# A hand-ordered attention schedule: weighing behind the copies, another order of products, a buffer for compressed-value weights

## The chip, the cores and the metric

The kernel runs on one core of a Trainium2 chip. Its time is the device time of one execution in microseconds (us); with one core there is nothing to take a maximum over. PE is TensorE, DVE is VectorE, ACT is ScalarE, POOL is GpSimd; SP issues the large loads.

## The reference, cut to what matters

256 tokens of width 1024, all in float32. First two layers of feed-forward, a mixer of two kinds of attention, feed-forward; then two layers of a hybrid attention and a feed-forward:

```python
def hybrid_mixer(h, w_in, ...):                 # "mixer"
    proj = h @ w_in                             # q, six key/value parts, gates, moba q k v
    kc = gelu(blocks(k_cmp) @ w_ck1) @ w_ck2    # compressed keys, values alike with w_cv1, w_cv2
    o_nsa  = g0 * attn(q, kc, vc) + g1 * attn(q_rot, k_slc, v_slc) + g2 * attn(q_rot, k_win, v_win)
    o_moba = attn(rope(q_m), rope(k_m), v_m)
    return concatenate([o_nsa, o_moba]) @ w_out

def hybrid_layer(x, ...):                       # "hybrid"
    aq, ak, av, iq, ik, iw, bq, bk, bv, gates = split_cols(rms_norm(x) @ w_in)
    ya = sparse_attention(rope(norm(aq)), rope(norm(ak)), av, top-k of an index score)
    yb = differential attention: (p0 - lam * p1) @ bv, then a norm
    x = x + (sigmoid(g_a) * (ya @ w_up_a) + sigmoid(g_b) * (yb @ w_up_b)) @ w_out
    return x + (silu(gate) * up) @ w_ffn_out
```

## The kernel before, in words

The activations stay on the chip, 314 MB of weights stream through it once. A weight chunk of 1 MB (512 input rows by 512 columns) is loaded by SP into one of three `raw` buffers; ACT rounds each half into `hi` and DVE forms `lo` as raw less hi (four buffers each); a product is then three matmuls, hi by the activation's high part, lo by high, hi by low (L210 to L212 in the mixers, L252 to L257 towards the residual, L312 and L316 in the feed-forward). A `raw` buffer is free for the next load once DVE has made the second `lo` of it. SP works its queue in order, so a load that waits for a buffer holds back all behind it.

In the feed-forward parts a scheduler orders the instructions. In the mixers (about 211 to 405 and 778 to 972 us of the trace) and the hybrids (1157 to 1395 and 1585 to 1825 us) the order on PE, ACT, DVE and POOL is that of the program's text (`manual_schedule`). There a list of products, `Fill` (L1580), is handed out between the steps of the attention: `fill.us(t)` issues products worth t us, by a planner's own figures; `fill.until(name)` issues them until the named product is done; `fill.later(t, f)` issues f when t us of the plan have gone by. `Fill.split` issues the roundings and the loads of the chunks ahead.

A mixer begins with `cmp_blocks` (L747), which copies compressed keys and values into `kd`, turns them on PE and adds positions into `fl`; `compress` (L781) multiplies `fl` by two loaded halves of w_ck1 and of w_cv1, in `raw` buffers, without rounding (L807). `keys` turns the selected and the window keys (`kt`), `heads_T` (L405) turns heads four at a time, `cmp_probs` (L865) makes the compressed attention's weights. Then `pipeline` (L500) walks over slots, 12 in a mixer and 8 in a hybrid (4 of differential attention, 4 of sparse). A slot has four steps:

- scores (`scores_exp`, L415): PE makes two score tiles and adds a mask; four times DVE takes a row maximum (`nm`, L436) and ACT the exponential (`P`, L439).
- weigh: DVE makes the factor `c` and scales `P` (L478, L479; in the differential slots L1271, L1272).
- turn (`p_T`, L443): PE transposes `P`, six times in a mixer slot; ACT copies two thirds to `PT` (L453), DVE one third (L458).
- values: PE multiplies `PT` by the values (L493, L495; in the differential slots from L1283).

The scores run two slots ahead of the values; `post` names further work behind a slot's values. In a round the old `pipeline` issues turn(n), products f1, values(n), post, scores(n+2), products f2, weigh(n+2), products f3.

## Time and profile before

| | |
|---|---|
| median of 3 runs | 2021.23 us (2019.96 to 2023.68) |
| the profiled execution's own time | 2026.66 us |
| its span | 2025.0 us |
| mean granted clock of PE | 0.960 |
| busy: PE, DVE, ACT, POOL | 1863.4, 1318.4, 1003.2, 577.3 us |
| loaded | 314 MB, 155 GB/s over the span |

The span is what the trace shows; the time also holds what lies around it (1.7 us here). PE is busy for 92% of the span, so 8% of it is what its waits can give, and the granted clock says how fast it was while busy: 1.00 is 2.4 GHz, 0.50 is 1.2 GHz. The rows that the prediction uses are quoted in a section of their own below.

### The profile page before, as it was taken

Reading aid. Unit: us, or ns where it says so; the run is one execution under the profiler, and the core shown is the slowest. Engines: PE = TensorE matmul, PEld = TensorE weight load, DVE = VectorE, ACT = ScalarE, POOL = GpSimd, SP = SyncE. Lnnn points to the kernel's source line nnn. Section 1 sums busy time; section 2 is a strip of 40 time slices with the busy share of each in tenths; the row PEclk is TensorE's granted clock in tenths of the full one; section 3 lists DMA queues with packets and bytes.
Section 4 is the critical chain, followed back from the end, with each engine's and each line's share of the span. In section 5 each row is a group of like instructions: output and inputs, shape, how many; then the busy total and the mean of one; then the engine's idle time right before and its main releaser. Section 6 shows DMA issues by size and latency. Waiting matters only on the chain.

```text
span 2025.0 us, 27057 instructions
## 1 busy us (share of the span) xinstructions
PE 1863.4 (92%) x10136; PEld 1547.9 (76%) x10136; DVE 1318.4 (65%) x2202; ACT 1003.2 (50%) x1948; POOL 577.3 (29%) x628
## 2 busy tenths in 40 slices
PE   8899788899999998878999998799999997899999
PEld 7788665688888887656888876687887776788887
DVE  7765445687667665346776588556866696567763
ACT  6554424555555554235655444445555444546552
POOL 5450110044315421100454144001542252013540
PEclk9899899999999999889999999899999998999999
DMA  7546432355655464412555544236546443245543
GB/s 247 184 146 210 153 120 63 105 187 157 228 177 175 159 229 148 147 42 83 189 178 182 184 137 145 84 105 208 167 145 229 152 146 104 84 162 193 169 164 125
DMA packets 149075, 314.40 MB, mean 155 GB/s; under 512 B 5588, under 2 KB 30320, under 8 KB 148944
## 3 DMA queue, kind: packets, MB, share of 16 engines
q1 hardware_dynamic: 148016, 311.15, 46.7%
q0 software_dynamic: 896, 1.52, 0.4%
q8 instruction: 79, 1.29, 0.3%
q14 instruction: 52, 0.43, 0.1%
q10 hardware_dynamic: 32, 0.01, 0.0%
HBM read 311.61 MB, written 1.05 MB: 154 GB/s over the span
## 4 chain that ended last, share of the span: by engine, by line
PE 65%; DVE 15%; ACT 9%; POOL 5%; issue 5%; DMA 2%; ACTq 0%; POOLq 0%; DVEq 0%
PE acc L312 10%; PE acc L253 7%; PE acc L257 7%; PE acc L252 7%; PE acc L316 5%; PE psS L312 5%; DVE lo L1578 4%; ACT P L439 3%; PE acc L210 3%; PE psT L312 2%; PE acc L212 2%; DVE lo L190 2%; PE acc L211 2%; PE psS L316 2%; PE psO L312 2%
## 5 line engine op out<-in xcount | busy, mean ns | idle before, releaser
L190 DVE TENSOR_TENSOR lo<-raw,hi 128x1024 fp32r<-128x1024 f32 (+2 forms) x436 | 535.3, 1254 | 158.6 <-ACT hi L189 153.7
L189 ACT ACTIVATE hi<-raw 128x1024 fp32r<-128x1024 f32 (+2 forms) x436 | 423.4, 999 | 150.0 <-PE acc L257 107.5
L312 PE MATMUL acc<-xx,hi 128*128 128x512 f32 x1056 | 376.8, 401 | 9.8 <-DVE gcol L139 7.4
L316 PE MATMUL acc<-xx,lo 128*128 128x256 f32 x1056 | 294.3, 281 | 0.0
L312 PEld LDWEIGHTS acc<-xx,hi 128*128 128x128 f32 x1056 | 199.6, 190 | 58.5 <-DVE gcol L139 7.7
L1578 DVE TENSOR_TENSOR lo<-raw,hi 128x1024 fp32r<-128x1024 f32 (+1 forms) x168 | 204.3, 1229 | 47.4 <-ACT hi L1577 47.2
L253 PE MATMUL acc<-lo,gh 128*128 128x512 f32 x528 | 209.7, 397 | 1.5 <-DVE lo L190 1.5
L252 PE MATMUL acc<-hi,gh 128*128 128x512 f32 x528 | 209.1, 396 | 0.0
L316 PEld LDWEIGHTS acc<-xx,lo 128*128 128x128 f32 x1056 | 200.6, 190 | 1.2
L312 PE MATMUL psS<-xx,hi 128*128 128x512 f32 x528 | 192.6, 398 | 2.2 <-ACT hi L189 2.2
L341 POOL TENSOR_TENSOR g<-g,rbc 128x256 f32<-128x256 f32 x132 | 136.0, 1044 | 181.8 <-DVE g L326 123.9
L353 POOL TENSOR_TENSOR hh<-g,u 128x256 f32<-128x256 f32 x132 | 138.0, 1053 | 162.1 <-DVE u L326 161.4
L257 PE MATMUL acc<-hi,gl 128*128 128x512 f32 x528 | 173.6, 395 | 0.0
L210 PE MATMUL acc<-hi,xx 128*128 128x512 f32 (+2 forms) x416 | 170.6, 411 | 1.6 <-ACT xx L1514 1.6
L1577 ACT ACTIVATE hi<-raw 128x1024 fp32r<-128x1024 f32 (+1 forms) x168 | 167.4, 1035 | 4.4 <-PE acc L212 4.2
L212 PE MATMUL acc<-hi,xx 128*128 128x512 f32 (+2 forms) x416 | 161.6, 388 | 0.8 <-DVE xx L1515 0.8
L211 PE MATMUL acc<-lo,xx 128*128 128x512 f32 (+2 forms) x416 | 161.3, 388 | 0.0
L351 POOL TENSOR_TENSOR g<-g,rbc 128x256 f32<-128x256 f32 x132 | 134.5, 1024 | 66.8 <-DVE g L344 66.8
L316 PE MATMUL psS<-xx,lo 128*128 128x256 f32 x528 | 149.2, 282 | 1.9 <-DVE lo L190 1.9
L223 ACT ACTIVATE gh<-hh 128x256 fp32r<-128x256 f32 x132 | 55.1, 418 | 172.4 <-POOL hh L353 172.1
L344 DVE SCALAR_TENSOR_TENSOR g<-th,g 128x256 f32<-128x256 f32 x132 | 82.4, 628 | 74.9 <-ACT th L343 74.9
L343 ACT ACTIVATE th<-g 128x256 f32<-128x256 f32 x132 | 54.8, 417 | 152.7 <-POOL g L341 152.4
(431 smaller groups left out, 3672.9 us busy)
## 6 DMA issues: line engine op xcount, KB each, us to landing
raw<-in_w_in_dram SPq DMA_DIRECT2D x60, 1024.0 KB, 5.1
raw<-in_w_ffn_down_dram SPq DMA_DIRECT2D x44, 1024.0 KB, 4.9
raw<-in_w_ffn_up_dram SPq DMA_DIRECT2D x40, 1024.0 KB, 5.1
raw<-in_w_ffn_in_dram SPq DMA_DIRECT2D x40, 1024.0 KB, 5.3
raw<-in_w_ffn_gate_dram SPq DMA_DIRECT2D x39, 1024.0 KB, 5.2
raw<-in_w_ffn_out_dram SPq DMA_DIRECT2D x22, 1024.0 KB, 5.1
raw<-in_w_out_dram SPq DMA_DIRECT2D x12, 1024.0 KB, 4.9
raw<-in_w_ffn_gate_dram SPq DMA_DIRECT2D x10, 512.0 KB, 3.8
```

Of the source, the lines that this page charges most:

```text
L189: nc.scalar.activation(hi[:, hs], raw[:, hs], AF.Copy),
L190: nc.vector.tensor_tensor(lo[:, hs], raw[:, hs], hi[:, hs].bitcast(F32), op=ALU.subtract),
L210: mm(out, ah, bh, start=start, stop=False)
L211: mm(out, ah, bl, start=False, stop=False)
L212: self.last = mm(out, al, bh, start=False, stop=stop)
L252: mm(accs[t, n], ah, hi[:, j, cs], start=k == 0, stop=False)
L253: mm(accs[t, n], ah, lo[:, j, cs], start=False, stop=False)
L257: mm(accs[t, n], al, hi[:, j, cs], start=False, stop=k == nk - 1)
L312: nc.tensor.matmul(banks[j], hi[:, k, fs], xk.rearrange("p u s -> p (u s)"), start=h == 0 and k == 0, stop=False,)
L316: self.last = nc.tensor.matmul(banks[j][:, 0:S], lo[:, k, fs], xk[:, 0, :], start=False, stop=h == 1 and k == 3,)
L1577: nc.scalar.activation(self.hi[:, hs], self.raw[:, hs], AF.Copy)
L1578: nc.vector.tensor_tensor(self.lo[:, hs], self.raw[:, hs], self.hi[:, hs].bitcast(F32), op=ALU.subtract)
```

## The change

`pipeline` now issues scores(n+1), products, then turn(n), weigh(n+1), products f1, values(n), post, scores(n+2), products f2: the weighing of the next slot stands behind this slot's copies of `PT` on DVE, where before the weighing of the slot after next stood ahead of the next slot's copies. The mixer projects `q` first and `kw` second (before: `kw`, `q`); the second key transpose and the second step of the compressed probabilities are done behind the first slot's scores (`pre`); the turns of `mq` and `mk` stand one slot later. w_cv1 gets a buffer of its own, `cv1`, one for both layers, and its first half is asked for before the hand-ordered part begins. In the hybrid `broadcast` is issued 8 us of the plan later, the index transposes 1 us later and with 3.2 us of products behind them instead of 2.0, the turns of `xa` 5 us later, those of `xk` behind the values of slots 0 and 1. Products whose inputs are not there yet are held back by a `ready` test instead of by their place. `Fill` looks 3 halves ahead at first and then 5 (before: 6). `kd`, `zr` and `pc` share one buffer instead of two, `u` shares that of `hs`, `e`. All instructions are the same in number on PE, DVE, ACT and POOL.

```diff
@@ -278,9 +278,10 @@
-        if fill:
+        if ready:
             return [
-                (None, [Chunk(self, rows(c), [2, D])], 16, lambda hl, c=c: run(c, hl[0]), None) for c in range(nch)
+                (None, [Chunk(self, rows(c), [2, D])], 16, lambda hl, c=c: run(c, hl[0]), None, lambda c=c: ready(c))
+                for c in range(nch)
             ], end
@@ -497,24 +498,31 @@
-    def pipeline(self, fill, slots, post, f1, f2, f3):
-        for n in range(2):
-            slots[n][0]()
-            fill.tick(0.85)
-            fill.us(2.2)
-            slots[n][1]()
-        fill.us(0.6)
+    def pipeline(self, fill, slots, post, f1, f2, pre=None):
+        slots[0][0]()
+        fill.tick(0.85)
+        fill.us(2.8)
+        if pre is not None:
+            pre()
+            fill.tick(0.2)
+            fill.us(0.7)
+        slots[0][1]()
+        slots[1][0]()
+        fill.tick(0.85)
+        fill.us(1.6)
         for n, (_, _, turn, values) in enumerate(slots):
...
             fill.tick(0.45 if rest else 0.65)
-            fill.us(f1)
             if rest:
+                fill.us(1.4)
                 rest()
                 fill.tick(0.2)
-                fill.us(0.9)
+            if n + 1 < len(slots):
+                slots[n + 1][1]()
+            fill.us(1.0 if rest else f1)
             values()
@@ -524,9 +532,6 @@
             fill.us(f2 - 0.4 if rest else f2)
-            if n + 2 < len(slots):
-                slots[n + 2][1]()
-            fill.us(f3 - 0.5 if rest else f3)
@@ -652,6 +657,7 @@
+                        tok["n"] = r + 1
@@ -660,13 +666,16 @@
+                def end(o):
+                    self.split(oh[:, 4 + k, :], ol[:, 4 + k, :], o[:, 0:256])
+                    tok["n"] = 5 + k
...
-                    self.caus, plain, self.psO,
-                    lambda o: self.split(oh[:, 4 + k, :], ol[:, 4 + k, :], o[:, 0:256]),
+                    self.caus, plain, self.psO, end,
@@ -682,64 +691,62 @@
             out, out_end = self.to_residual(
-                lambda k: oh[:, k, :], lambda k: ol[:, k, :], out_rows, KT, 1.0, after, held=1, fill=True
+                lambda k: oh[:, k, :], lambda k: ol[:, k, :], out_rows, KT, 1.0, after, held=1,
+                ready=lambda c: tok.get("n", 0) >= 2 * c + 2 or c == 3,
             )
             fill = Fill([
+                self.proj_item("q", w_in, 0, 512, pr, queries),
                 self.proj_item("kw", w_in, 1024, 280, pr, windows),
-                self.proj_item("q", w_in, 0, 512, pr, queries),
                 self.proj_item("mq", w_in, 1304, 512, pr, moba_in("mq", True)),
                 self.proj_item("mk", w_in, 1816, 512, pr, moba_in("mk", True)),
...
             fill.prime()
+            next(comp)
             es.enter_context(tc.manual_schedule(engines=MANUAL))
             rope2(kv[:, :, 256:384])
...
             fill.us(2.5)
             next(blocks)
-            fill.until("kw")
+            fill.us(1.6)
             next(blocks, None)
-            next(comp)
-            fill.us(4.5)
+            fill.us(3.6)
             next(comp)
             fill.until("q")
...
             fill.us(0.7)
             next(kt_)
-            fill.us(0.7)
-            next(kt_)
             qT, qrT, mq, mk = (mp.tile([128, 4, S], F32, tag="T4", name=n, bufs=4) for n in ("qT", "qrT", "mqT", "mkT"))
-            fill.us(0.7)
+            fill.us(1.1)
             q = tok["q"]
             self.heads_T(qT, q, 0, self.psT, 0.125)
...
             q4 = q.rearrange("p t (h d) -> p t h d", h=8)
             self.rope_part(mp, q4, q4, 8)
-            fill.us(1.0)
+            fill.us(2.0)
             next(comp)
             next(comp)
             fill.us(1.2)
             next(comp)
-            fill.us(2.6)
+            fill.us(1.8)
+            fill.until("kw")
             next(comp, None)
             self.heads_T(qrT, q, 0, self.psT, 0.125)
             self.heads_T(qrT, q, 1, self.psO, 0.125)
-            fill.us(1.0)
             probs = self.cmp_probs(mp, cp, qT, kcb, gt, tok)
-            next(probs)
-            fill.us(1.2)
+            fill.us(0.7)
             next(probs)
...
             post = {
                 0: lambda: next(probs, None),
-                2: lambda: self.heads_T(mq, tok["mq"], 0, self.psT, 0.125),
-                3: lambda: self.heads_T(mq, tok["mq"], 1, self.psT, 0.125),
-                4: lambda: self.heads_T(mk, tok["mk"], 0, self.psT),
-                5: lambda: self.heads_T(mk, tok["mk"], 1, self.psT),
+                3: lambda: self.heads_T(mq, tok["mq"], 0, self.psT, 0.125),
+                4: lambda: self.heads_T(mq, tok["mq"], 1, self.psT, 0.125),
+                5: lambda: self.heads_T(mk, tok["mk"], 0, self.psT),
+                6: lambda: self.heads_T(mk, tok["mk"], 1, self.psT),
             }
-            self.pipeline(fill, slots, post, 1.3, 1.1, 0.8)
+            self.pipeline(fill, slots, post, 1.8, 1.4, lambda: (next(probs), next(kt_)))
             fill.all()
             es.close()
@@ -747,17 +754,14 @@
-        kds = []
...
-            kd = mp.tile([128, 2, 2, 2, 64], F32, tag="c2", name="kd", bufs=2)
+            kd = mp.tile([128, 2, 2, 2, 64], F32, tag="c2", name="kd")
...
-            kds.append(kd)
-        for i, kd in enumerate(kds):
@@ -791,10 +795,10 @@
         def fetch(h):
-            return [
-                self.wraw(a[n][l][h * 1024 : (h + 1) * 1024, :].rearrange("(j p) f -> p j f", p=128), [8, 256])
-                for n in ("w_ck1", "w_cv1")
-            ]
+            src = [a[n][l][h * 1024 : (h + 1) * 1024, :].rearrange("(j p) f -> p j f", p=128) for n in ("w_ck1", "w_cv1")]
+            w = mp.tile([128, 8, 256], F32, name="cv1", bufs=1)
+            nc.sync.dma_start(w, src[1])
+            return [self.wraw(src[0], [8, 256]), w]
@@ -823,7 +827,7 @@
-        u = mp.tile([128, 128], F32, name="u")
+        u = mp.tile([128, 256], F32, tag="hs", name="u")[:, 0:128]
@@ -843,7 +847,7 @@
-        zr = mp.tile([128, 2, 2, 2, 32], F32, tag="c2", name="zr", bufs=2)
+        zr = mp.tile([128, 2, 2, 2, 32], F32, tag="c2", name="zr")
@@ -892,7 +896,7 @@
-        pc = cp.tile([128, 2, 8, 32], F32, tag="c2", name="pc", bufs=2)
+        pc = cp.tile([128, 2, 8, 32], F32, tag="c2", name="pc")
@@ -1078,7 +1082,6 @@
             ix = evac(ps, 324, "ix")
-            pr.broadcast()
             ikd = mp.tile([128, 2, 2, 64], F32, name="ikd")
@@ -1343,11 +1346,11 @@
                 fs = slice(f % 4, f % 4 + 2)
-                self.split(mh[f // 4][:, fs, :], ml[f // 4][:, fs, :], m)
+                fill.later(2.0, lambda: self.split(mh[f // 4][:, fs, :], ml[f // 4][:, fs, :], m))
...
                 lambda k: mh[k // 4][:, k % 4, :], lambda k: ml[k // 4][:, k % 4, :], a["w_out_2"][l], KT,
-                0.5, after, held=1, fill=True,
+                0.5, after, held=1, ready=lambda c: True,
             )
@@ -1361,21 +1364,23 @@
                 gate(1, 1, lambda: gate_b(1)),
-                up(ub, 0, lambda: tok["ybh"], lambda: tok["ybl"], up_b),
-                up(ub, 1, lambda: tok["ybh"], lambda: tok["ybl"], up_b),
-                up(ua, 0, lambda: yah, lambda: yal, up_a),
-                up(ua, 1, lambda: yah, lambda: yal, up_a),
+                up(ub, 0, lambda: tok["ybh"], lambda: tok["ybl"], up_b, lambda: "y" in tok),
+                up(ub, 1, lambda: tok["ybh"], lambda: tok["ybl"], up_b, lambda: "y" in tok),
+                up(ua, 0, lambda: yah, lambda: yal, up_a, lambda: "ya" in tok),
+                up(ua, 1, lambda: yah, lambda: yal, up_a, lambda: "ya" in tok),
             ] + out)
...
             es.enter_context(tc.manual_schedule(engines=MANUAL))
+            fill.later(8.0, pr.broadcast)
             fill.later(2.5, lambda: index_rope(0))
...
             fill.until("xb")
+            fill.us(1.0)
             index_T()
             fill.tick(0.65)
-            fill.us(2.0)
+            fill.us(3.2)
             for _ in index_scores():
@@ -1389,20 +1394,24 @@
             fill.until("xk")
-            fill.us(1.0)
+            fill.us(6.0)
             self.heads_T(aqT, tok["xa"], 0, self.psT, 0.125)
...
             fill.until("bv")
-            fill.us(0.5)
-            self.heads_T(akT, tok["xk"], 0, self.psT)
-            self.heads_T(akT, tok["xk"], 1, self.psO)
             slots = [diff(h) for h in range(4)] + [sparse(k) for k in range(4)]
-            self.pipeline(fill, slots, {3: norm_y}, 1.3, 1.3, 1.3)
+            post = {
+                0: lambda: self.heads_T(akT, tok["xk"], 0, self.psT),
+                1: lambda: self.heads_T(akT, tok["xk"], 1, self.psT),
+                3: norm_y,
+            }
+            self.pipeline(fill, slots, post, 1.8, 1.8)
             fill.us(2.0)
...
                 fill.tick(0.45)
-                fill.us(1.2)
+                if t == 0:
+                    fill.us(1.2)
+            tok["y"] = tok["ya"] = True
             fill.all()
@@ -1589,12 +1598,12 @@
             self.upto.append(self.upto[-1] + 2 * len(it[1]))
-        self.pos, self.now, self.debt = 0, 0.0, 0.0
+        self.pos, self.ahead, self.now, self.debt = 0, 3, 0.0, 0.0
         self.i, self.gen, self.n, self.past, self.tasks = 0, None, 0, set(), []
...
         while self.pos < min(upto, len(self.halves)):
-            for c, _ in self.halves[self.pos : self.pos + 6]:
+            for c, _ in self.halves[self.pos : self.pos + self.ahead]:
                 c.ask()
@@ -1602,6 +1611,7 @@
         self.split(self.upto[1])
+        self.ahead = 5
@@ -1640,17 +1652,20 @@
         self.debt += t
-        while self.debt > 0 and self.step():
-            pass
+        while self.debt > 0:
+            if not self.step():
+                self.tick(self.debt)
+                self.debt = 0.0
...
         while name not in self.past:
-            self.step()
+            assert self.step()
         self.debt = 0.0
...
             pass
+        assert self.i == len(self.items)
         self.tick(1e9)
```

On SP, in the mixer of layer 0 (`raw` from in_w_in is a chunk of the projections, 280 columns for `kw`, from in_w_ck and in_w_cv a half of a compression weight). Before:

```order
L175 DMA raw<-in_w_in_dram 128x4x280 x2
L175 DMA raw<-in_w_in_dram 128x4x512 x5
L175 DMA raw<-in_w_ck_dram 128x8x256
L175 DMA raw<-in_w_cv_dram 128x8x256
L175 DMA raw<-in_w_ck_dram 128x8x256
L175 DMA raw<-in_w_cv_dram 128x8x256
L175 DMA raw<-in_w_in_dram 128x4x512 x3
```

and now:

```order
L175 DMA raw<-in_w_in_dram 128x4x512 x4
L175 DMA raw<-in_w_in_dram 128x4x280
L175 DMA raw<-in_w_ck_dram 128x8x256
L175 DMA raw<-in_w_in_dram 128x4x280
L175 DMA raw<-in_w_in_dram 128x4x512 x2
L800 DMA cv_2233<-in_w_cv_dram 128x8x256
L175 DMA raw<-in_w_ck_dram 128x8x256
L175 DMA raw<-in_w_in_dram 128x4x512 x4
```

The first half of w_ck1 moved ahead of the second chunk of `kw` and of both chunks of `mq`; the second halves (L800 and the row behind it) now stand behind the two chunks of `mq`. The first half of w_cv1 is gone from here: it is SP's seventh load at the start of the program, between two loads of the first feed-forward; that of layer 1 stands among the loads of w_out of layer 0.

On DVE, in slots of the mixer of layer 0 in which moba heads are turned (`nm` belongs to scores, `c` and `P` to weigh, `PT` to turn, `lo` to the next product's chunk, `ol` to the slot's result). Before:

```order
L458 COPY PT<-psO 128x2x128
L1578 TENSOR_TENSOR lo<-raw,hi 128x1024
L224 TENSOR_TENSOR ol<-psO,oh 128x256
L436 TENSOR_REDUCE nm<-psS 128x1 x4
L635 TENSOR_SCALAR c<-sm 128x4
L636 RECIPROCAL c<-c 128x4
L478 TENSOR_SCALAR P<-P,c 128x256 x2
L479 TENSOR_TENSOR P<-P,c 128x2x128
L458 COPY PT<-psO 128x2x128
```

and now:

```order
L459 COPY PT<-psO 128x2x128
L640 TENSOR_SCALAR c<-sm 128x4
L641 RECIPROCAL c<-c 128x4
L479 TENSOR_SCALAR P<-P,c 128x256 x2
L480 TENSOR_TENSOR P<-P,c 128x2x128
L224 TENSOR_TENSOR ol<-psO,oh 128x256
L437 TENSOR_REDUCE nm<-psS 128x1 x4
L1587 TENSOR_TENSOR lo<-raw,hi 128x1024
L459 COPY PT<-psO 128x2x128
```

Between the maxima `nm` and the next copy `PT` stood the four rows of the weighing; now one rounding, `lo`, stands there, and the weighing behind the copy.

On PE, in the hybrid of layer 0, the turns of `xk` and the scores behind them (L428 and L430 before, L429 and L431 now). Before:

```order
L212 MATMUL acc<-hi,xx 128x512
L410 MATMUL psT<-ident,xk 128x128 x4
L410 MATMUL psO<-ident,xk 128x128 x4
L428 MATMUL psS<-bkT,bqT 128x256 x2
L430 MATMUL psS<-bkT,bqT 128x128 x2
```

and now:

```order
L1286 MATMUL psO<-tok,PT 128x128
L1287 MATMUL psO<-tok,PT 128x128
L1288 MATMUL psO<-tok,PT 128x128
L411 MATMUL psT<-ident,xk 128x128 x4
L429 MATMUL psS<-bkT,bqT 128x256 x2
L431 MATMUL psS<-bkT,bqT 128x128 x2
```

The turns stood ahead of the first slot; each of the two now follows the values of a slot.

## Rows read from the trace of the kernel before

**Rows 1.** The page's first part: busy time, share of the span, instructions of each engine.

```profile
PE 1863.4 (92%) x10136; PEld 1547.9 (76%) x10136; DVE 1318.4 (65%) x2202; ACT 1003.2 (50%) x1948; POOL 577.3 (29%) x628
```

**Rows 2.** Four stretches: us, busy PE PEld DVE ACT POOL, PE clock, DMA share, GB/s.

```profile
239.20:252.90 13.70, 6.21 (x36) 3.10 (x37) 1.10 (x1) 0.00 (x0) 0.00 (x0) 0.50 0.53 164
283.00:400.00 117.00, 92.79 (x503) 66.69 (x503) 65.59 (x163) 54.00 (x145) 4.89 (x8) 0.91 0.25 77
1239.30:1246.20 6.90, 5.41 (x15) 4.49 (x16) 6.53 (x12) 2.88 (x5) 4.21 (x6) 0.51 0.48 158
1261.00:1330.00 69.00, 52.94 (x349) 45.48 (x348) 39.18 (x100) 32.80 (x101) 1.85 (x2) 0.88 0.21 69
```

**Rows 3.** What PE waited for, 211 to 405 us: us, times, longest.

```profile
PE psO L493 <- DVE PT L458: 16.1, 6, 4.9
PE psS L807 <- DMA raw<-in_w_ck_dram: 9.2, 1, 9.2
PE psS L807 <- DMA raw<-in_w_cv_dram: 2.9, 1, 2.9
```

**Rows 4.** The same, 778 to 972 us.

```profile
PE psS L807 <- DMA raw<-in_w_ck_dram: 9.1, 1, 9.1
```

**Rows 5.** The same, 1150 to 1395 us.

```profile
PE psO L1283 <- DVE PT L458: 10.6, 4, 4.7
PE psO L493 <- DVE PT L458: 5.1, 3, 2.6
PE psS L1130 <- ACT iT L1114: 2.6, 1, 2.6
PE psO L410 <- DVE xa L1005: 2.2, 1, 2.2
PE psO L410 <- DVE xk L1005: 2.2, 1, 2.2
PE psT L410 <- DVE xa L1005: 1.6, 1, 1.6
```

**Rows 6.** Timeline of DVE in one mixer slot: start, us, line, operation, [idle before].

```profile
332.65 0.29 DVE L436 TENSOR_REDUCE nm<-psS 128x1 f32<-128x128 f32 x1 [0.65 <-ACT P L439]
334.41 1.23 DVE L1578 TENSOR_TENSOR lo<-raw,hi 128x1024 fp32r<-128x1024 f32 x1 [1.47 <-ACT hi L1577]
335.55 0.16 DVE L635 TENSOR_SCALAR c<-sm 128x4 f32<-128x4 f32 x1
337.02 0.42 DVE L458 COPY PT<-psO 128x256 f32<-128x256 f32 x1
```

**Rows 7.** Timeline of ACT in the same slot.

```profile
333.33 1.04 ACT L1577 ACTIVATE hi<-raw 128x1024 fp32r<-128x1024 f32 x1
334.28 0.57 ACT L453 COPY PT<-psT 128x512 f32<-128x512 f32 x1
```

**Rows 8.** Timeline of PE, products at either clock.

```profile
1245.51 0.63 PE L210 MATMUL acc<-hi,xx 128*128 128x512 f32 x1
1245.94 0.50 PE L211 MATMUL acc<-lo,xx 128*128 128x512 f32 x1
1246.51 0.40 PE L210 MATMUL acc<-hi,xx 128*128 128x512 f32 x1
1246.75 0.40 PE L211 MATMUL acc<-lo,xx 128*128 128x512 f32 x1
```

**Rows 9.** Timeline of SP's queue, layer 0 mixer.

```profile
238.06 0.37 SPq L175 DMA_DIRECT2D raw<-in_w_ck_dram  x1
240.33 0.37 SPq L175 DMA_DIRECT2D raw<-in_w_cv_dram  x1
```

**Rows 10.** DMA issues, 190 to 280 us: xcount, KB each, median us to landing.

```profile
raw<-in_w_in_dram SPq DMA_DIRECT2D x8, 1024.0 KB, 5.2
```

**Rows 11.** DMA from 0 to 34 us: rate in 40 equal slices, and one group of issues.

```profile
GB/s 0 0 194 274 296 357 371 376 293 256 374 400 388 367 386 386 392 225 207 267 217 142 164 181 222 255 236 405 405 417 373 337 280 65 14 0 0 0 101 311
raw<-in_w_ffn_up_dram SPq DMA_DIRECT2D x3, 1024.0 KB, 11.1
```

More of the change, by code (lines that the diff above doesn't have):

```diff
@@ L229, in ft, with to_residual @@
         return (self.psS, self.psT, self.psS, self.psO)[self.n_ft % 4]()
-    def to_residual(self, yh, yl, w, nk, scale, after, held=2, fill=False):
+    def to_residual(self, yh, yl, w, nk, scale, after, held=2, ready=None):
         nc = self.nc
@@ L382, in run @@
             done(ps)
-        return name, chunks, 16, run, None
+        return name, chunks, 16, run, None, None
     def proj(self, w, c0, n, xh, xl):
@@ L1220, in run, with up @@
                             )
-                return f"g{i}{c}", chunks, 32, run, None
-            def up(w, c, yh, yl, done):
+                return f"g{i}{c}", chunks, 32, run, None, None
+            def up(w, c, yh, yl, done, ready):
                 chunks = [Chunk(self, w[:, c * 512 : (c + 1) * 512].rearrange("(k p) f -> p k f", p=128), [4, 512])]
@@ L1241, in run @@
                         done(4 * c + 2 * j, ps.rearrange("p (f s) -> p f s", f=2))
-                return None, chunks, 16, run, None
+                return None, chunks, 16, run, None, ready
             def sparse(k):
@@ L1620, in step @@
             return False
-        name, chunks, steps, run, done = self.items[self.i]
+        name, chunks, steps, run, done, ready = self.items[self.i]
+        if ready is not None and not ready():
+            return False
         if self.gen is None:
```

## The prediction

> **What bounds the kernel now.** I read the page's busy times first [rows 1]: PE is busy 1863 us of 2025, the next engine, DVE, 1318. So PE bounds the kernel, and a change that takes no matmul away can only give back PE's idle time, some 160 us, and what PE loses at a low clock. Then I looked at where that idle time lies. The change reorders the two mixers and the two hybrids and adds one load at the start, so I asked what PE waited for there. In a mixer [rows 3] there are two kinds: two long waits for the compression weights, 9.2 and 2.9 us, ended by a DMA, and six waits of the values for DVE's third of `PT`, 16.1 us together. Layer 1 is alike [rows 4]. In a hybrid [rows 5] the values wait for the same copy, 10.6 us in four differential slots and 5.1 in three sparse ones; ahead of the slots the turns of `xa` and `xk` wait for DVE's rotation, 2.2, 1.6 and 2.2 us, and the index scores 2.6. Third, the stretches [rows 2]: the 12 slots of a mixer take 117 us with PE busy for 92.8, so 24.2 idle; the 8 slots of a hybrid 69 with 52.9, so 16.1 idle. Behind the longest waits the granted clock falls to 0.50, which is 1.2 GHz: 13.7 us after the wait for w_ck1, 6.9 us at the turns of `xa`, and the slots run at 0.91 and 0.88 in the mean. What that costs is in PE's own timeline [rows 8]: consecutive product matmuls start 0.43 us apart in the low stretch and 0.24 behind it, so low-clock work takes nearly twice its time.
>
> Why the copy is late is in DVE's timeline of one slot [rows 6] and ACT's [rows 7]: the last maximum ends at 332.94, ACT's rounding begins at 333.33 and takes 1.04, DVE's `lo` 1.23, then from 335.55 to 337.02 the weighing of a later slot, and only then the copy. The weighing is 1.47 us of that queue, and nothing in it is needed for the values that wait.
>
> **The change, part by part.** The sum is made against the profiled execution, 2026.66 us; the median of the runs is 5.4 us lower, and I take that off at the end.
>
> *Compression weights.* Before, SP issues the first halves at 238.06 and 240.33 [rows 9], when `raw` buffers come free behind two products, and PE stands still until they land. Now the first half of w_cv1 has been there since long before, and that of w_ck1 stands ahead of the second chunk of `kw`; a load of 1 MB takes 5.2 us to land [rows 10], and PE reaches it behind most of the 16 triples of a product (three matmuls of 0.24 us each [rows 8], 11.5 us for all). Both waits go: 12.1 us in layer 0, 11.9 in layer 1 (its first is 9.1 [rows 4]; the second I take as a little under 2.9), **-24**. With them goes the low stretch behind them: 6.21 us of PE work at half clock [rows 2] would take 3.1, twice, **-6.2**.
>
> The second halves are new in their place. SP may issue that of w_cv1 only when PE has read the first one out of the only buffer, and that of w_ck1 stands behind it and behind two chunks of `mq`. Third of three loads at the highest rates the trace shows, about 400 GB/s [rows 11], that is 2.6 us for 1.05 MB: 5.2 + 2 x 2.6 = 10.4 us. PE's cover until it wants them is the rest of `q` (11.5 us less the 7.7 that the code hands out before, 3.8) and the 0.7, 1.1 and 2.0 us of products in the code: 7.6 us and ten transposes. That leaves a wait of 2.8 if the three are issued together, none if the buffers come free earlier, 6 if `mq`'s rounding holds them longer: I take 3 each, by the sum just made, **+6**, and half of the low stretch again, 1.5 each, **+3**. One buffer for `kd` makes the second copy wait for the first turn, and the copies stand behind the additions of `fl` on DVE: nothing to 2 us, 1 each, **+2**.
>
> *Start.* The first half of w_cv1 is a seventh large load where the rate is 256 to 400 GB/s, from slice 5 to 17, and an up load takes 11.1 us to land [rows 11]. The loads behind it come up to 2.6 us later; later in that window the rate falls to 142, so part is made good: 0 to 2.6, I take **+1**. The load for layer 1 lies among those of w_out of layer 0, where SP waits for buffers anyway and `cv1` has long been read: nothing; without that cover it is again one load, 2.6.
>
> *Slots of the mixers.* Each of the six waits is shorter by the weighing, 1.47 us: 9 us each. Against it stand two waits that move in. The window keys' `kt` copy now stands on DVE behind the probabilities and a `lo`, and slot 1's scores need it; the nearest row is the longest wait of that stretch, 4.9 [rows 3]. And the last turn of `mk` is now directly ahead of the scores that read it; nearest is the 1.6 of the turns of `xa` [rows 5]. 9 - 4.9 - 1.6 = 2.5, **-5** for both. Ends: -9 each with nothing given back, 0 with all of it.
>
> *Ahead of the slots of the hybrids.* The turns of `xa` come 5 us later in the plan, longer than their waits of 1.6 + 2.2; those of `xk`, 2.2, follow values for which their rotation is long done. 6.0 us each, **-12**, and 5.41 us of low-clock work at 0.51 [rows 2] becomes 2.8, **-5.2**. The index turn gets 1 us more of cover and 1.2 more behind it, against 2.6 in layer 0: **-2**. The copies of the `xk` turns go into slots 0 and 1 on ACT and DVE, where they stand ahead of the maxima; I count them with the slots. The later broadcast hides beside products: nothing.
>
> *Slots of the hybrids.* Seven waits, each shorter by 1.5: 10.5. Against it: slot 0 is weighed directly ahead of its turn, with a `lo` in between (nearest, the second xa wait, 2.2), and in slot 5 a rounding, two gate evacuations and four tanh stand between the scores and the copies (nearest, the longest wait, 4.7). 10.5 - 2.2 - 4.7 = 3.6, **-7** for both. Ends 0 and -10.5 each.
>
> The `ready` tests and the shorter look-ahead change no order that PE waits on; the cover is that three `raw` buffers allow no more loads ahead than that, and without it one load is late by 2.6 us.
>
> Sum: -24 - 6.2 + 6 + 3 + 2 + 1 - 5 - 12 - 5.2 - 2 - 7 = -49.4. 2026.66 - 49.4 = 1977.3; less 5.4, **1972**.
>
> **The rivals.** A: *the slots give nothing.* The `lo`s and evacuations still stand between maxima and copies, and 12 us of the sum are lost: 1984. For it: ACT's rounding and DVE's `lo` are 2.3 of the 4 us between maxima and copy [rows 6, 7]; against: the 1.47 that goes is as plain.
>
> B: *the slots' gaps come from tiles that ran out*, so that order alone doesn't move them. The waits end with the copy itself and not with a read that frees a bank [rows 3, 5], which speaks against it; the time would be that of A, 1984. The Trainium skill, Perfetto Trace Analysis, "Optimization Strategy", reads a gap that repeats over a stretch as a possible sign that SBUF or PSUM has no room for the next tile; by that rule, the slots would keep 24.2 and 16.1 us.
>
> C: *nothing is given back.* The second halves land in time (9 us) and none of the new waits shows (13 in the mixers, 14 in the hybrids): 1972 - 36 = 1936. For it, DVE is busy only 65.6 of 117 us and 39.2 of 69 in the slots [rows 2]; against, its order is fixed and it waits for ACT.
>
> D: *the clock.* Many short waits in place of a few long ones could hold PE low through whole slot stretches. PE's work there at 0.75 instead of 0.91 and 0.88 takes 92.8 x 0.91/0.75 = 112.6 and 52.9 x 0.88/0.75 = 62.1, 19.8 and 9.2 more, 58 for two layers: 1972 + 58 = 2030, slower. It turns at about 0.77. Against it: the low stretches seen so far follow waits of 2 us and more, and those get fewer.
>
> E: *it all cancels*, the waits only change their names: 2021.
>
> **How the numbers follow.** Forecast 0.50, A 0.18, B 0.04, C 0.17, D 0.07, E 0.04. 0.2% is 4 us, about what a measurement of this kernel can tell from no change. Forecast, A, B and C are faster by more: 0.89; E is the same, 0.04; D slower, 0.07. The range takes in A and B with a start and second halves at their worst (1.6 and 6 more, and some us of error in the slots): 2000, and C with a little of the clock regained in the slots: 1930. D, E and the better half of C's tail are left out.
>
> **What would show it.** In the changed profile: no DMA wait of PE at w_cv1's first half or w_ck1's; a wait of about 3 us at the second half of w_ck1; no waits at the turns of `xa` and `xk`; `PT` waits of some 7 us instead of 16.1 in a mixer, with one on `kt` of 4 to 5; in slot 5 of the hybrids the longest wait. I am wrong if the slots of the mixers still have 24 us idle (A, B), if the second halves are never waited for (C), or if the clock of the slot stretches falls under 0.8 (D).

## The result, and the profile after

The changed kernel takes 1994.05 us (median of 4 runs, 1991.70 to 1996.09), the kernel before 2022.3 beside it: ratio 0.986, 95% interval 0.984 to 0.988, so 28 us less where 49 were forecast. The profiled span fell from 2025.0 to 1991.0 us, 34 us: the profiled execution was 4.4 us above the median before and 1.3 below it after, so some 6 of the 34 us are a difference between executions. One of e1's ten executions, at 2967.82 us and a mean clock of 0.556, is left out of its figures. The page's busy times after, beside [rows 1]:

```profile
PE 1850.7 (93%) x10136; PEld 1540.6 (77%) x10136; DVE 1322.6 (66%) x2202; ACT 1004.0 (50%) x1948; POOL 581.4 (29%) x628
```

PE does the same 10136 matmuls in 12.7 us less busy time, so at a better clock (mean 0.969 instead of 0.960; busy time times mean clock is nearly the same, 1789 and 1793 us); the other 21.3 us are idle time.

The stretches of layer 0, cut at the same PE instructions in both kernels: first turn of `kd`, first scores of the mixer, first product of the next feed-forward; then first index turn, first scores of the hybrid, first turn of `yb`. Columns: us; busy time of PE, PEld, DVE, ACT, POOL, each with its instructions; PE's clock, DMA share, GB/s. Before:

```profile
225.20:279.40 54.20, 40.02 (x245) 30.46 (x243) 22.71 (x40) 14.50 (x20) 7.41 (x17) 0.84 0.53 177
279.40:400.20 120.80, 96.09 (x523) 69.08 (x522) 68.23 (x173) 55.01 (x148) 4.89 (x8) 0.92 0.25 75
1178.20:1257.40 79.20, 69.46 (x348) 56.37 (x346) 68.30 (x123) 34.83 (x51) 44.41 (x37) 0.91 0.45 146
1257.40:1340.00 82.60, 66.53 (x453) 57.69 (x453) 46.27 (x112) 38.84 (x114) 1.85 (x2) 0.90 0.27 89
```

After:

```profile
226.90:267.80 40.90, 31.32 (x217) 25.10 (x215) 16.44 (x34) 10.27 (x16) 6.47 (x15) 0.87 0.54 181
267.80:389.80 122.00, 101.09 (x559) 73.57 (x558) 75.69 (x182) 60.11 (x154) 6.10 (x10) 0.94 0.31 93
1161.70:1227.30 65.60, 62.07 (x329) 50.79 (x327) 59.98 (x112) 30.23 (x45) 37.59 (x33) 1.00 0.47 156
1227.30:1310.40 83.10, 65.22 (x433) 54.79 (x433) 54.35 (x121) 41.91 (x118) 7.95 (x6) 0.88 0.27 90
```

Idle is a stretch's length less PE's busy time. In the front of the mixer it fell from 14.2 to 9.6, in its slots from 24.7 to 20.9, ahead of the hybrid's slots from 9.7 to 3.5 with the clock at 1.00 instead of 0.91. But in the hybrid's slots it rose, from 16.1 to 17.9. Work moved across the cuts with the key turns, so the lengths are compared over whole stages of the profiled executions, in us, from the first of these cuts to the first product of the next feed-forward:

| | mixer 0 | mixer 1 | hybrid 0 | hybrid 1 | all else |
|---|---|---|---|---|---|
| before | 175.0 | 173.4 | 223.2 | 217.5 | 1235.9 |
| after | 162.9 | 165.6 | 213.3 | 209.0 | 1240.2 |

What PE waited for in the mixer of layer 0 after the change (us in total, times, longest; the rows used below), to be read beside [rows 3]:

```profile
PE psO L494 <- DVE c L640: 5.1, 2, 3.0
PE psS L429 <- DVE kt L625: 4.4, 1, 4.4
PE psS L811 <- DMA raw<-in_w_ck_dram: 4.3, 1, 4.3
PE psS L842 <- issue: 3.2, 1, 3.2
PE psT L458 <- ACT PT L454: 2.7, 4, 1.1
PE acc L252 <- ACT hi L1586: 2.5, 2, 1.3
PE acc L253 <- DVE lo L1587: 1.5, 2, 0.8
PE psO L496 <- DVE PT L459: 1.5, 1, 1.5
PE psS L429 <- DVE mkT L417: 1.4, 1, 1.4
PE psS L858 <- issue: 1.4, 1, 1.4
```

The 9.2 and 2.9 us for the compression weights are gone. In their place the second half of w_ck1 is waited for (4.3), the second compression product for `z` and the next for `zr` (L842 and L858, 3.2 and 1.4), and slot 1's scores for the `kt` copy (4.4). The products with w_out (L252, L253) wait 4.0 us for their rounding, 4.5 in the mixer of layer 1, a wait that neither the kernel before nor e5 below has. The values' waits for DVE's copy are 5.1 and 1.5 where they were 16.1; the trace names `c`, the row just behind that copy, as releaser. In the hybrid, beside [rows 5]:

```profile
PE psS L429 <- ACT P L440: 7.0, 1, 7.0
PE psO L494 <- ACT PT L454: 4.8, 1, 4.8
PE psO L1286 <- DVE c L1184: 4.8, 2, 2.4
PE psS L1133 <- ACT iT L1117: 1.3, 1, 1.3
```

The waits at the turns of `xa` and `xk` are gone, but slot 1's scores (L429) wait 7.0 us for slot 0's exponentials. DVE shows why (start, us, line, operation, [idle before]):

```profile
1231.99 1.75 DVE L1009 TENSOR_TENSOR xk<-t,hr 128x512 f32<-128x512 f32 x1 [1.05 <-POOL hr L204]
1233.66 2.28 DVE L1587 TENSOR_TENSOR lo<-raw,hi 128x1024 fp32r<-128x1024 f32 x1
1235.86 0.68 DVE L1009 TENSOR_TENSOR xk<-t,hr 128x512 f32<-128x512 f32 x1
1236.47 1.21 DVE L1587 TENSOR_TENSOR lo<-raw,hi 128x1024 fp32r<-128x1024 f32 x1
1237.60 0.41 DVE L437 TENSOR_REDUCE nm<-psS 128x1 f32<-128x256 f32 x1
```

And POOL:

```profile
1228.99 2.96 POOL L204 TENSOR_TENSOR hr<-hv,neghalf 128x16 f32<-128x16 f32 x1
1233.27 1.59 POOL L1002 TENSOR_TENSOR t<-t,t 128x512 f32<-128x512 f32 x1
```

The last step of `xk`'s rotation, in two halves on DVE, waits 1.05 us for POOL's `hr`. The second half stands behind a `lo` of 2.28 us; POOL's `t`, which it reads too, had ended at 1234.9, before that `lo` did. Behind them stands another `lo`, and then the first maximum of slot 0, at 1237.60. Slot 0's scores had been on PE at 1227.3. Before, PE waited for the same chain at the turns of `xk`.

### The profile page after: what moved, and what is told of

Read it like the earlier page. It is cut to its first block, busy times and chain, and to the rows that moved or that the text cites. A ratio compares the mean times of both kernels' runs of the same rounds, so it can differ in the third digit from the quotient of the medians.

```text
span 1991.0 us, 27090 instructions
## 1 busy us (share of the span) xinstructions
PE 1850.7 (93%) x10136; PEld 1540.6 (77%) x10136; DVE 1322.6 (66%) x2202; ACT 1004.0 (50%) x1948; POOL 581.4 (29%) x628
## 3 DMA queue, kind: packets, MB, share of 16 engines
HBM read 311.61 MB, written 1.05 MB: 157 GB/s over the span
## 4 chain that ended last, share of the span: by engine, by line
PE 52%; DVE 20%; ACT 12%; POOL 7%; issue 6%; DMA 2%; SPq 0%; ACTq 0%; POOLq 0%; DVEq 0%
PE acc L253 7%; PE acc L257 7%; PE acc L252 7%; PE acc L313 6%; DVE lo L190 6%; DVE lo L1587 4%; ACT P L440 3%; ACT hi L189 3%; PE acc L317 3%; PE psS L313 3%; POOL hh L354 2%; PE acc L210 2%; POOL g L342 2%; PE acc L212 2%; PE acc L211 2%
## 5 line engine op out<-in xcount | busy, mean ns | idle before, releaser
L1587 DVE TENSOR_TENSOR lo<-raw,hi 128x1024 fp32r<-128x1024 f32 (+1 forms) x168 | 209.4, 1257 | 61.3 <-ACT hi L1586 61.2
L253 PE MATMUL acc<-lo,gh 128*128 128x512 f32 x528 | 209.3, 396 | 2.7 <-DVE lo L190 2.7
L252 PE MATMUL acc<-hi,gh 128*128 128x512 f32 x528 | 210.0, 398 | 0.0
L212 PE MATMUL acc<-hi,xx 128*128 128x512 f32 (+2 forms) x416 | 161.8, 389 | 2.1 <-DVE xx L1524 2.1
```

The costliest lines, as they stand in the source:

```text
L212: self.last = mm(out, al, bh, start=False, stop=stop)
L252: mm(accs[t, n], ah, hi[:, j, cs], start=k == 0, stop=False)
L253: mm(accs[t, n], ah, lo[:, j, cs], start=False, stop=False)
L1587: nc.vector.tensor_tensor(self.lo[:, hs], self.raw[:, hs], self.hi[:, hs].bitcast(F32), op=ALU.subtract)
```

## The experiments

Each was timed in 3 rounds against the kernel before on the same chip. Ratios are to that kernel. The figures by stage and the rows are of one profiled execution each.

**e1: the order of the weighing undone.** In each round of `pipeline`:

```diff
-            if n + 1 < len(slots):
-                slots[n + 1][1]()
             fill.us(1.0 if rest else f1)
             values()
...
             fill.us(f2 - 0.4 if rest else f2)
+            if n + 2 < len(slots):
+                slots[n + 2][1]()
```

(and the weighing of slot 1 ahead of the first round.)

> The changed kernel with one part undone: in each round of the slots the weighing of the slot after next is again issued behind its scores and the products, ahead of the next turn; amounts of products, posts and all else as changed. Theory (the weighing between maxima and copy made the copy late): the waits of the values for the PT copies come back, some 2.5 us a mixer and 3.5 a hybrid and a little clock, so about 12 to 18 us over the changed kernel's 1994, near 2008. Rival (the slots gained from the moved turns and the amounts of products, not from this order): within 4 us of 1994.

Measured: 2024.81 us, ratio 1.000 (0.998 to 1.001). The whole gain is gone: 31 us over the changed kernel, where 12 to 18 were expected. The waits of the mixer of layer 0 and the page's busy times:

```profile
PE psO L494 <- DVE PT L459: 12.0, 5, 3.8
PE 1864.9 (92%) x10136; PEld 1551.4 (77%) x10136; DVE 1323.8 (65%) x2202; ACT 1002.1 (50%) x1948; POOL 581.6 (29%) x628
```

In the mixer the copy is waited for 12.0 us in all, against 5.1. Against the changed kernel the span is 32.1 us longer (2023.1), of which 14.2 are PE's busy time (1864.9 against 1850.7) and 17.9 its idle time: nearly half of what the order is worth is clock. Over all executions the mean clock was 0.961 to 0.967 here and 0.969 to 0.972 in the changed kernel. By stages, the mixers are 10.4 and 6.9 us longer than in the changed kernel and the hybrids 10.4 and 8.3.

**e5: that order alone, in the kernel before.** The same edit the other way round, in the old `pipeline` with its amounts.

> The kernel before with only the weighing moved behind the next slot's copies, amounts of products, front of the mixer, loads and turns as before. Theory (the order of the weighing makes nearly the whole gain, and the other parts cancel): about 1995, ratio 0.984 to 0.989. Rival (the order pays only together with the moved turns and amounts): half the gain or less, 2008 or more.

Measured: 1990.34 us, ratio 0.985 (0.983 to 0.987), no worse than the whole change. The waits for the compression weights are all there, and the values' waits are short (the last row is the page's busy times):

```profile
PE psS L808 <- DMA raw<-in_w_ck_dram: 9.3, 1, 9.3
PE psO L493 <- DVE c L636: 6.4, 2, 3.4
PE 1843.3 (93%) x10136; PEld 1532.0 (77%) x10136; DVE 1318.1 (66%) x2202; ACT 1003.1 (50%) x1948; POOL 579.6 (29%) x628
```

The slots of the mixer and of the hybrid, same columns as above:

```profile
280.50:385.90 105.40, 90.94 (x523) 65.83 (x522) 66.74 (x171) 54.47 (x146) 4.89 (x8) 0.95 0.27 80
1227.60:1308.00 80.40, 66.21 (x453) 56.84 (x453) 46.06 (x112) 38.81 (x114) 1.85 (x2) 0.92 0.28 91
```

The mixer's slots take 105.4 us instead of 120.8: 10.2 less idle, and 5.2 less busy at 0.95 instead of 0.92. The hybrid's take 80.4 instead of 82.6. By stages: mixers 161.8 and 159.4, hybrids 218.5 and 214.0. So in the kernel before the order is worth some 27 us in the mixers and 8 in the hybrids; in the changed kernel, by e1, it is 17 and 19. The other parts of the change, together, are worth nothing that was measured; with them the hybrids are 5 us shorter each than here, and the mixers 1 and 6 longer.

**e2: the rotation of xk behind the first slots' maxima.**

```diff
-for d, f in zip(((1.2, 2.8, 6.8), (3.6, 5.2, 8.0))[t], steps):
+for d, f in zip(((1.2, 2.8, 16.0 if name == "xk" else 6.8), (3.6, 5.2, 18.5 if name == "xk" else 8.0))[t], steps):
...
-    0: lambda: self.heads_T(akT, tok["xk"], 0, self.psT),
-    1: lambda: self.heads_T(akT, tok["xk"], 1, self.psT),
+    1: lambda: self.heads_T(akT, tok["xk"], 0, self.psT),
+    2: lambda: self.heads_T(akT, tok["xk"], 1, self.psT),
```

> The changed kernel with the last step of the rotation of xk issued behind the maxima of slots 1 and 2 on DVE, and the turns of xk one slot later each. Theory (the rotation, which waits for POOL, stands ahead of the first slot's maxima, and that is the new wait of 7.0 us at the second slot's scores): that wait falls to 3 us or less in both hybrids, and the time to about 1984, 8 us of idle time and 2 to 4 of clock less. Rival (PE simply has too few products between the first two slots' scores, or the rotation's wait reappears whole at the turns of xk): no gain, 1990 to 1998.

Measured: 1997.06 us, ratio 0.988 (0.986 to 0.990). Waits in the hybrid of layer 0:

```profile
PE psO L494 <- ACT PT L454: 4.2, 1, 4.2
PE psS L429 <- ACT P L440: 3.6, 1, 3.6
PE psO L1286 <- DVE c L1184: 3.6, 2, 2.7
PE psS L429 <- DVE akT L417: 3.0, 1, 3.0
```

The wait fell to 3.6 us in both hybrids, where the theory had 3 or less, but 3.0 us appeared at the scores that read `akT`, whose turn is now directly ahead, and the time did not fall: the hybrids take 216.6 and 210.9 us, 3.3 and 1.9 longer than in the changed kernel. Much of the wait was for the rotation; taking it out of that place of the queue paid nothing by itself. The rival's time was right.

**e3: the kt copy ahead of the probability chain.**

```diff
-self.pipeline(fill, slots, post, 1.8, 1.4, lambda: (next(probs), next(kt_)))
+self.pipeline(fill, slots, post, 1.8, 1.4, lambda: (next(kt_), next(probs)))
```

> The changed kernel with the window keys' second turn issued ahead of the second step of the compressed probabilities, so that the kt copy stands ahead of that chain on DVE. Theory (the 4.4 us wait of slot 1's scores is the chain ahead of the copy): the wait falls to about 1 us in both mixers, and with the clock behind it the time to about 1985. Rival (the chain only moves its wait to the first turn, since the first weighing stands behind it): 1992 to 1996, with a new wait of about the same size at the first turn.

Measured: 1987.87 us, ratio 0.983 (0.981 to 0.986), about 6 us less than the change, though the two intervals overlap (0.984 to 0.988 for the change). The wait was halved, not removed; a `lo` and the maxima still stand ahead of the copy, and the first turn waits 0.9 for the weighing:

```profile
PE psS L429 <- DVE kt L625: 2.1, 1, 2.1
```

**e4: z ahead of kw's evacuations.**

```diff
         nc.vector.scalar_tensor_tensor(z, u, 1.0, z, op0=ALU.add, op1=ALU.mult)
+        yield
...
             next(comp)
+            next(comp)
             fill.us(1.8)
             fill.until("kw")
```

> The changed kernel with the last step of the compression's gelu (z) issued on DVE right behind the tanh, ahead of the rounding and the evacuations of kw. Theory (the wait of the second compression product, 3.2 us against 1.3 before the change, is longer because kw is now finished just there, with its evacuations ahead of z): the wait falls to about 1 us, twice 2 us and some clock, 1988 to 1991. Rival (it is the tanh's own latency): 3.2 us stays, 1994.

Measured: 1992.87 us, ratio 0.985 (0.983 to 0.987). The wait at the product that reads `z` is gone, and that of the next one, which reads `zr`, grew from 1.4 to 4.4, since the copies into `zr` still stood behind:

```profile
PE psS L860 <- issue: 4.4, 1, 4.4
```

Neither theory said that. It settles that the tanh is not what is waited for; it gained nothing.

**e6: the second half of w_ck1 asked for early.** `compress` asks for it behind the first half, in a step of its own that the mixer calls behind the first turn of `kd`:

```diff
+        ck = self.wraw(part("w_ck1", 1), [8, 256])
+        yield
...
-                ws = fetch(1)
+                ws = [ck, fetch_v(1)]
```

> The changed kernel with the load of the second half of w_ck1 asked for right behind that of its first half, ahead of the second chunk of kw and of mq; that of w_cv1 stays. Theory (the 4.3 us wait is the load's place, third of three): the wait falls under 1 us in both mixers, with the clock behind it about 1984 to 1988. Rival (the loads of kw and mq come later for it and the products run dry): the same 1994 with a new wait at a product.

Measured: 1994.46 us, ratio 0.986 (0.984 to 0.988): no gain. The wait for w_ck1's second half is gone, so it had been for the place of that load; but the wait for w_cv1's second half stands where it was, 0.3 us shorter. The rows of SP's queue, the first of the changed kernel and the next two of e6, show why:

```profile
236.34 0.50 SPq L800 DMA_DIRECT2D cv<-in_w_cv_dram  x1
240.32 0.37 SPq L175 DMA_DIRECT2D raw<-in_w_in_dram  x1
240.74 0.50 SPq L803 DMA_DIRECT2D cv<-in_w_cv_dram  x1
PE psS L817 <- DMA cv<-in_w_cv_dram: 4.0, 1, 4.0
```

In both kernels PE had read the first half out of `cv1` by 236.3. In e6 the load of the second half was still issued 4.4 us later, behind a load for the projections that was held until 240.32, while the second half of w_ck1, asked for early, held one of the three `raw` buffers. So it is SP's queue, and not the one buffer of w_cv1, that makes it late here; the expectation of e10 names the buffer. The rival was right in the time, and the new wait is at the compression and not at a product of `Fill`.

In the changed kernel SP had issued the load of w_ck1 at 236.90 (row below), and PE began at 248.48: 11.6 us for the 10.4 of the forecast. The forecast counted two loads ahead of it; the trace has three under way when it was issued (two for the projections from 234.2 and 235.5, and that of w_cv1).

```profile
236.90 1.86 SPq L175 DMA_DIRECT2D raw<-in_w_ck_dram  x1
```

**e7: no buffer of its own for w_cv1.**

```diff
-            w = mp.tile([128, 8, 256], F32, name="cv1", bufs=1)
-            nc.sync.dma_start(w, src[1])
-            return [self.wraw(src[0], [8, 256]), w]
+            return [self.wraw(p, [8, 256]) for p in src]
```

> The changed kernel without the buffer of its own: both halves of w_cv1 go through the raw buffers, each behind that of w_ck1, and no load is added at the start. Theory (the buffer spares SP's queue two loads where they count): the start gives back 1 to 3 us, but the waits at the first or second halves grow by 4 or more in each mixer, so 1998 to 2006. Rival (asking early is worth it only for the first halves, and projecting q first does that alone): 1990 to 1994.

Measured: 1995.33 us, ratio 0.986 (0.983 to 0.989). The buffer saves 2.2 us of waiting in the mixer of layer 0 (3.7 and 2.8 here, 4.3 with it), and that mixer begins 2.1 us later with it (226.9 against 224.8); the rival is right within the interval, and the theory's 4 us and more a mixer were not there. Projecting q first hides the first halves alone.

```profile
PE psS L809 <- DMA raw<-in_w_ck_dram: 3.7, 1, 3.7
PE psS L809 <- DMA raw<-in_w_cv_dram: 2.8, 1, 2.8
```

**e8: three of these waits together.** e3 and e6, and z as in e4 with its two copies into `zr` moved ahead as well:

```diff
+        zr = mp.tile([128, 2, 2, 2, 32], F32, tag="c2", name="zr")
+        nc.gpsimd.memset(zr, 0.0)
+        for m in range(2):
+            nc.vector.tensor_copy(zr[:, m, :, :, 0:16], ...)
+        yield
         ps = self.psS()
```

> Three edits of the changed kernel together: the kt copy ahead of the probability chain (as in e3), the second half of w_ck1 asked for early (as in e6), and z with its two copies into zr ahead of the rounding and kw's evacuations (e4 moved z alone, and the wait went on to zr). Theory (each is a wait of its own on PE): 6 us from the first, 6 to 8 from the second, 4 from the third, about 1977. Rival (waits in one stage replace each other): no better than e3, 1986 to 1990.

Measured: 1976.75 us, ratio 0.978 (0.976 to 0.979), the time that was forecast. The sum behind it did not hold: the second term, 6 to 8 us, did not come, since a wait for the compression weights of the same size stayed, as in e6. The waits for `z` and `zr` are down to 0.2 us from 4.6 in each mixer, those for `kt` to 2.1 and 2.0 from 4.4, and the mixers are 6.2 and 11.0 us shorter than in the changed kernel, of it 5.9 and 4.8 idle time. That the time came out is luck in part. For the compression weights and the keys there are left

```profile
PE psS L818 <- DMA cv<-in_w_cv_dram: 4.1, 1, 4.1
PE psS L429 <- DVE kt L625: 2.1, 1, 2.1
```

**e9: cover ahead of the hybrid's slots.** e8 and one line:

```diff
             fill.until("bv")
+            fill.us(5.0)
             slots = [diff(h) for h in range(4)] + [sparse(k) for k in range(4)]
```

> e8 with one more edit: 5 us more of products in the hybrids between the product of bv and the first slot's scores. Theory (the 7.0 us wait of slot 1's scores is the rotation of xk ahead of slot 0's maxima, a chain of fixed length that PE reaches too early): the wait falls to about 2 us in both hybrids, with the clock behind it 10 us less than e8, about 1967. Rival (as in e2, what goes there comes back in the slots, which now have fewer products): within 4 us of e8's 1977.

Measured: 1969.43 us, ratio 0.974 (0.972 to 0.976), 7 us less than e8 (timed on another chip, beside the same kernel before). The wait of slot 1's scores fell from 7.0 to

```profile
PE psS L429 <- ACT P L440: 2.6, 1, 2.6
```

and alike in layer 1. That this is where the 7 us come from is not shown. The profiled span is 8.5 us shorter than that of e8, but the hybrids only 0.4 and 2.0: in their slots the idle time fell by 2.9 and 2.5, ahead of the slots it rose by 2.8 and 1.1. The other 6 us lie in the mixers and between the stages, which the edit does not reach.

**e10: cover ahead of the second half of the compression.** e9 and

```diff
             self.rope_part(mp, q4, q4, 8)
-            fill.us(2.0)
+            fill.us(5.5)
```

> e9 with one more edit: 5.5 instead of 2.0 us of products ahead of the second half of the compression. Theory (its wait of 4.1 us, now for w_cv1, whose only buffer is free too late, is covered by as much): the wait falls to under 1 us and 5 to 8 us with the clock are gained over e9, about 1960. Rival (products used up there are missed in the slots, or mq's chunks are late): within 4 us of e9.

Measured: 1950.62 us, ratio 0.965 (0.963 to 0.967), 19 us less than e9 where 5 to 8 were expected, and the best version: 43 us less than the change under study. In the mixer of layer 0 the wait for w_cv1 fell to 0.4 us and that for `kt` to 0.5 (in layer 1 to nothing and 2.1). Its longest groups of waits are now

```profile
PE psT L458 <- ACT PT L454: 3.9, 3, 1.4
PE psO L494 <- DVE c L640: 2.6, 1, 2.6
PE psO L494 <- ACT PT L454: 1.9, 5, 0.5
PE psS L857 <- issue: 1.5, 1, 1.5
```

The mixers take 146.1 and 142.6 us, in e9 154.8 and 154.7; their idle time fell by 4.9 and 7.8. The hybrids are within 0.5 us of e9. With the products moved, the rounding and the evacuations of kw also came ahead of `z` and of the first slot's maxima; how much of the 19 us is the wait and how much this was not separated.

## Why the prediction was right or wrong, point by point

The range held the time and the direction was right; the size was some 1.7 times too large (49 for 28). By its own steps, in the profiled executions, where 49.4 us were forecast and the span fell 34: of the 15 us that are missing, the hybrids have 8 (18.4 us shorter for 26.2), the mixers 4 (19.9 for 24.2) and all else 3 (4.3 longer for 1).

- *Compression weights.* Both waits went. The second halves cost 4.3 us in layer 0 and 3.9 in layer 1, for a forecast of 3 each, by the mechanism named; `kd` 0.65 each, for 1. What failed is what the step left out: `fill.until("kw")` moved kw's evacuations between the tanh and `z`, and the waits at L842 and L858 grew to 3.2 and 1.4 from these rows of the kernel before:

```profile
PE psS L838 <- issue: 1.3, 1, 1.3
PE psS L854 <- PE psS L838: 0.7, 1, 0.7
```

  The idle time of the front fell by 4.6 and 4.8, not by 8 each. e4 and e8 show that these evacuations were the cause.
- *Start.* Forecast +1. The mixer of layer 0 begins 1.7 us later; right. Of the other 2.6 us by which all else is longer, 2.3 lie between the mixer of layer 1 and the first hybrid; in e2 to e4 that stretch is as short as before, so they are not a steady cost of the change.
- *Slots of the mixers.* Forecast -5 with 4.9 for `kt` and 1.6 for `mk` given back. The idle time fell by 3.8 and 3.0, `kt` cost 4.4 and `mk` 1.4. The size was right, and e5 shows the 9 us of gain without the give-back: 10.2. But the step counted no clock, and in e5 that is another 5 us in one mixer's slots; and the sum took it that the `ready` tests and the shorter look-ahead "change no order that PE waits on", while the products with w_out now wait 4.0 and 4.5 us for their rounding. Which part of the change brought that wait was not tested. So the size came out in part by luck.
- *Ahead of the hybrids' slots.* This is the step that failed: "those of `xk`, 2.2, follow values for which their rotation is long done". It asked when the turns would come and not what stands behind the rotation on DVE. The idle time ahead of the slots fell by 6.2 and 6.3, near the 8.0 and 6.0 forecast, but the delay went on to the next in DVE's queue, slot 0's maxima, and PE waits 7.0 us for them in each hybrid. Over the whole hybrids the idle time fell by 7.8 us where 21 were forecast; the busy time fell by 10.6 for 5.2, and so the clock hides a part of the miss. What this wait alone is worth stays open: e2 halved it and e9 took it to 2.6 us, and the hybrids came out 3.3 and 1.9 us longer and 0.4 and 2.0 shorter.
- *Slots of the hybrids.* Forecast -7. Without that 7.0 the idle time in them fell by 5.2 and 5.6. Slot 5's wait is 4.8 for the 4.7 assumed, the longest but for that 7.0, which the signs did not name.
- *The attribution.* The sum gave a quarter of the gain to the weighing's order net and most to loads and turns. e1 and e5 turn this round: the order alone gives all of it. Before the new waits were set against it, the sum had 39 us for the order, all of it idle time (9 and 10.5 us, twice), against 28 to 32 measured, of which 17.9 and 17.2 are idle time in the profiled executions of e1 and e5; and it had 10 us for all other parts together, against nothing measured. It hid this by setting the new waits of the other parts against the order's gain.

Of the rivals, A and B did not come: e5 changes the order alone, with every buffer as before, and the mixer's slots lose 10.2 of 24.7 us of idle time. The Trainium skill, Perfetto Trace Analysis, "Optimization Strategy", says that a gap which repeats can mean that there is no room for the next tile; for these 10.2 us the trace does not agree. D did not come: the slots' clock rose in the mixers from 0.92 to 0.94, and stayed near in the hybrids, 0.90 and 0.88. C's waits showed, but for the 2.2 us at the first turn of a hybrid; e8 and e10 shortened most of those in the mixers, by order and by cover.

## What to carry to other kernels

On an engine that works in order, put behind a copy that PE waits for whatever nobody waits for yet: here that one move gave the whole gain. When a wait is taken off a chain, ask what is queued next behind the chain on the same engine, for that is where it comes back: here 2.2 us at the turns of `xk` became 7.0 at the next scores. Giving PE other work for the length of a wait made the mixers 8.7 and 12.1 us shorter in e10, but in e9 it took a wait from 7.0 to 2.6 us and the hybrids became only 0.4 and 2.0 shorter; so look at the whole stage and not at the one wait. And try each part of a large change alone, both by taking it out and by putting it in by itself: parts that look like half of the gain may cancel.

## What had not been expected of the hardware

About half of what the order was worth was PE's clock: between e1 and the changed kernel the same matmuls took 1864.9 and 1850.7 us of busy time, at mean granted clocks of 0.962 and 0.969, beside 17.9 us of idle time. Busy time times clock is 1794 and 1793 us, so the clock accounts for the difference. Between the kernel before and e5 it is 20.1 us of busy time, at 0.960 and 0.971, beside 17.2 us of idle time. The forecast priced the clock only where it saw one long wait go, and forecast 8.4 us of it in all; the busy time fell 12.7.
